# Two rows per partition, stores on a second queue, and last stores behind last loads in a windowed attention kernel

## Chip, cores, metric

One core of one Trainium2 chip. The metric is device time in microseconds (us) of one execution; each time below is the median of several executions unless it says otherwise. The runs s1 to s5 have one execution each; their times are given, but the argument reads them by their trace.

## The reference

Attention inside windows of 64 rows, in fp32. Four batches of 4,096 rows, 1,536 columns.

```python
B, S, D, W = 4, 4096, 1536, 64
q_w, k_w, v_w = (x.reshape(B, S // W, W, D) for x in (q, k, v))
logits = np.einsum('bnwd,bnud->bnwu', q_w, k_w) * D ** -0.5
attn = softmax(logits, axis=-1)                  # [cut: written out with max, exp, sum]
out = np.einsum('bnwu,bnud->bnwd', attn, v_w).reshape(B, S, D)
```

## The kernel before

It works through 128 blocks of 128 rows (two windows). Each partition holds one row. The GpSimd queue casts q, k and v from fp32 to fp16 while it loads them: one descriptor per row reads 6,144 B from HBM and writes 3,072 B to SBUF. A descriptor is the order to move one run of bytes, here one row; the trace shows one packet for each (65,536 rows in all, 65,536 data packets). Each DMA (one `dma_start`) also shows 16 completion writes of 4 B (8,192 for 512 DMAs), one for each DMA engine. TensorE transposes q and k, multiplies them, and multiplies the exponentials with v in two concurrent 64x64 quarters of the array. The stores are also issued by GpSimd, two blocks late; only the last three go through SP.

```python
    def load(blk):
        # [cut: the tiles q16, k16, v16, 3 buffers each]
        nc.gpsimd.dma_start(out=q16, in_=qb[blk].rearrange("p (c e) -> p c e", e=128))
        nc.gpsimd.dma_start(out=k16, in_=kb[blk].rearrange("p (c e) -> p c e", e=128))
        nc.gpsimd.dma_start(out=v16, in_=vb[blk])
        return q16, k16, v16
    ...
    for blk in range(NBLK):
        # [cut: first blocks are loaded ahead]
        q16, k16, v16 = load(blk)
        if len(pending_store) > 2:
            bs, ts = pending_store.pop(0)
            nc.gpsimd.dma_start(out=ob[bs], in_=ts)
        # [cut: 24 transposes, copies to SBUF]
        for c in range(DC):
            nc.tensor.matmul(lt[:, 0:128], lhsT=xt[:, 2 * c + 1, :], rhs=xt[:, 2 * c, :],
                             start=(c == 0), stop=(c == DC - 1))
        # [cut: exponentials of the two windows, row sums, reciprocal]
        for j in range(D // 512):
            nc.tensor.matmul(o[0:64, :], lhsT=et[0:64, 0:64], rhs=v16[0:64, sl], tile_position=(0, 0), ...)
            nc.tensor.matmul(o[64:128, :], lhsT=et[64:128, 64:128], rhs=v16[64:128, sl], tile_position=(64, 64), ...)
            # [cut: eviction with the reciprocal as scale]
        pending_store.append((blk, out_sb))
    for bs, ts in pending_store:
        nc.sync.dma_start(out=ob[bs], in_=ts)
```

The softmax here doesn't subtract the row's maximum and nothing guards it: scores larger than these inputs give would overflow.

Of the kernel before, what the change touches and what calls it, by code (L numbers as in the profile page):

```python
# [1 line left out]

# [4 lines left out]

FP16 = mybir.dt.float16
FP32 = mybir.dt.float32  # L10


@with_exitstack
def kernel(
    ctx: ExitStack,
    tc: tile.TileContext,
    q: bass.AP,
    k: bass.AP,
    v: bass.AP,
    out: bass.AP,  # L20
):
    nc = tc.nc

    B, S, D, W = q.shape[0], q.shape[1], q.shape[2], 64
    P = 128
    DC = D // 128
    NBLK = (B * S) // P
    scale = float(D) ** -0.5
    NPRE = 2

    qb = q.rearrange("b (n p) d -> (b n) p d", p=P)
    kb = k.rearrange("b (n p) d -> (b n) p d", p=P)
    vb = v.rearrange("b (n p) d -> (b n) p d", p=P)
    ob = out.rearrange("b (n p) d -> (b n) p d", p=P)

    consts = ctx.enter_context(tc.tile_pool(name="consts", bufs=1))
    inp = ctx.enter_context(tc.tile_pool(name="inp", bufs=3))
    xtp = ctx.enter_context(tc.tile_pool(name="xtp", bufs=2))
    etp = ctx.enter_context(tc.tile_pool(name="etp", bufs=2))
    outp = ctx.enter_context(tc.tile_pool(name="outp", bufs=6))  # L40
    rsp = ctx.enter_context(tc.tile_pool(name="rsp", bufs=2))

    tp_ps = ctx.enter_context(tc.tile_pool(name="tp_ps", bufs=2, space=bass.MemoryType.PSUM))
    lt_ps = ctx.enter_context(tc.tile_pool(name="lt_ps", bufs=2, space=bass.MemoryType.PSUM))
    o_ps = ctx.enter_context(tc.tile_pool(name="o_ps", bufs=3, space=bass.MemoryType.PSUM))
    s_ps = ctx.enter_context(tc.tile_pool(name="s_ps", bufs=1, space=bass.MemoryType.PSUM))

    exp_f = mybir.ActivationFunctionType.Exp
    copy_f = mybir.ActivationFunctionType.Copy

    def load(blk):
        q16 = inp.tile([128, DC, 128], FP16, tag="q16", name="q16")
        k16 = inp.tile([128, DC, 128], FP16, tag="k16", name="k16")
        v16 = inp.tile([128, D], FP16, tag="v16", name="v16")
        nc.gpsimd.dma_start(out=q16, in_=qb[blk].rearrange("p (c e) -> p c e", e=128))  # L55
        nc.gpsimd.dma_start(out=k16, in_=kb[blk].rearrange("p (c e) -> p c e", e=128))  # L56
        nc.gpsimd.dma_start(out=v16, in_=vb[blk])  # L57
        return q16, k16, v16

    pre = [load(blk) for blk in range(NPRE)]  # L60
    pending_store = []

    ident = consts.tile([128, 128], FP16, name="ident")
    ones = consts.tile([128, 8], FP16, name="ones")
    zeros = consts.tile([128, 1], FP32, name="zeros")
    nc.vector.memset(ident, 0.0)
    nc.vector.memset(ones, 1.0)
    nc.vector.memset(zeros, 0.0)
    nc.gpsimd.affine_select(
        out=ident,  # L70
        in_=ident,
        compare_op=mybir.AluOpType.not_equal,
        fill=1.0,
        base=0,
        pattern=[[-1, 128]],
        channel_multiplier=1,
    )

    for blk in range(NBLK):
        if blk < NPRE:  # L80
            q16, k16, v16 = pre[blk]
        else:
            q16, k16, v16 = load(blk)
        if len(pending_store) > 2:
            bs, ts = pending_store.pop(0)
            nc.gpsimd.dma_start(out=ob[bs], in_=ts)  # L86

        xt = xtp.tile([128, 2 * DC, 128], FP16, tag="xt", name="xt")
        for g in range(3):
            tp = tp_ps.tile([128, 8, 128], FP16, tag="tp", name="tp")  # L90
            for i in range(8):
                j = g * 8 + i
                c = j // 2
                src = q16[:, c, :] if (j % 2 == 0) else k16[:, c, :]
                nc.tensor.transpose(tp[:, i, :], src, ident)  # L95
            if g != 1:
                nc.vector.tensor_copy(out=xt[:, g * 8 : g * 8 + 8, :], in_=tp)  # L97
            else:
                nc.scalar.copy(out=xt[:, g * 8 : g * 8 + 8, :], in_=tp)  # L99

        lt = lt_ps.tile([128, 512], FP32, tag="lt", name="lt")
        for c in range(DC):
            nc.tensor.matmul(  # L103
                lt[:, 0:128],
                lhsT=xt[:, 2 * c + 1, :],
                rhs=xt[:, 2 * c, :],
                start=(c == 0),
                stop=(c == DC - 1),
            )

        et = etp.tile([128, 128], FP16, tag="et", name="et")
        nc.scalar.activation(  # L112
            et[0:64, 0:64], lt[0:64, 0:64], exp_f, bias=zeros[0:64], scale=scale
        )
        nc.scalar.activation(
            et[64:128, 64:128], lt[64:128, 64:128], exp_f, bias=zeros[64:128], scale=scale
        )

        sp = s_ps.tile([128, 8], FP32, tag="sp", name="sp")
        nc.tensor.matmul(  # L120
            sp[0:64, 0:1], lhsT=et[0:64, 0:64], rhs=ones[0:64, 0:1],
            tile_position=(0, 0), start=True, stop=True,
        )
        nc.tensor.matmul(  # L124
            sp[64:128, 0:1], lhsT=et[64:128, 64:128], rhs=ones[64:128, 0:1],
            tile_position=(64, 64), start=True, stop=True,
        )
        rs = rsp.tile([128, 1], FP32, tag="rs", name="rs")
        nc.vector.reciprocal(out=rs, in_=sp[:, 0:1])  # L129

        out_sb = outp.tile([128, D], FP32, tag="out_sb", name="out_sb")
        for j in range(D // 512):
            o = o_ps.tile([128, 512], FP32, tag="o", name="o")
            sl = slice(512 * j, 512 * (j + 1))
            nc.tensor.matmul(  # L135
                o[0:64, :], lhsT=et[0:64, 0:64], rhs=v16[0:64, sl],
                tile_position=(0, 0), start=True, stop=True,
            )
            nc.tensor.matmul(  # L139
                o[64:128, :], lhsT=et[64:128, 64:128], rhs=v16[64:128, sl],  # L140
                tile_position=(64, 64), start=True, stop=True,
            )
            if j % 2 == 0:
                nc.scalar.activation(out_sb[:, sl], o, copy_f, bias=0.0, scale=rs)  # L144
            else:
                nc.vector.tensor_scalar_mul(out_sb[:, sl], o, scalar1=rs)  # L146

        pending_store.append((blk, out_sb))

    for bs, ts in pending_store:  # L150
        nc.sync.dma_start(out=ob[bs], in_=ts)


# [1 line left out]
_INS = ['q', 'k', 'v']  # L155
_OUTS = [((4, 4096, 1536), 'float32')]


# [23 lines left out]
```

## Time and profile before

| | before |
|---|---|
| time, median of 3 (the result below has a fourth run) | 967.0 us (966.24 to 967.76) |
| profiled span | 964.4 us |
| TensorE busy, granted clock | 76%, 0.63 |
| bytes read and written in HBM | 302 MB, 101 MB |

The page of the kernel before: busy time of each engine; two rows of 40 time slices (granted TensorE clock and DMA busy share, in tenths); DMA packets; packets, MB and busy share by queue; HBM traffic; the chain of waits by engine. Queue q0 is GpSimd's, q1 is SP's, q8 is an instruction queue.

```profile
span 964.4 us, 14246 instructions
...
PE 731.4 (76%) x5632; PEld 510.0 (53%) x5632; DVE 294.6 (31%) x515; ACT 378.1 (39%) x641; POOL 271.1 (28%) x514
...
PEclk9776575756756666566575755766656556565655
DMA  9999999999999999999999999999999999999997
...
DMA packets 73795, 252.60 MB, mean 262 GB/s; under 512 B 8192, under 2 KB 8192, under 8 KB 73728
...
q0 software_dynamic: 73296, 249.33, 104.6%
q1 hardware_dynamic: 432, 2.36, 0.6%
q8 instruction: 44, 0.72, 0.3%
...
HBM read 301.99 MB, written 100.66 MB: 417 GB/s over the span
...
DMA 94%; issue 4%; PE 1%; POOL 0%; DVE 0%; ACT 0%; POOLq 0%; ACTq 0%; DVEq 0%
```

Read the DMA row first: 9 in every slice but the last, and the chain that ended last is 94% DMA. Then the counts. The 73,795 packets hold 65,536 data packets (65,152 on q0 and 384 on q1); most of the others are 8,192 completion writes of 4 B. The packet sizes are those of the SBUF side, so HBM traffic is larger than the "252.60 MB".

The table of stretches, with columns start:end and length, then busy us and count of each engine, then granted clock, DMA share, GB/s:

```profile
core 0: us, PE busy (x) PEld busy (x) DVE busy (x) ACT busy (x) POOL busy (x), PEclk, DMA share, GB/s
...
100.00:900.00 800.00, 620.30 (x4719) 432.69 (x4720) 246.28 (x429) 315.63 (x535) 227.99 (x429) 0.62 1.07 265
...
940.00:950.00 10.00, 8.40 (x61) 5.59 (x60) 2.95 (x6) 3.62 (x7) 0.54 (x1) 0.50 1.05 283
950.00:957.00 7.00, 4.50 (x37) 3.19 (x33) 1.92 (x3) 2.39 (x3) 0.00 (x0) 0.51 0.73 242
957.00:965.00 8.00, 1.76 (x15) 0.63 (x12) 1.13 (x3) 1.89 (x4) 0.00 (x0) 0.70 0.30 122
```

The DMA share is 1.07 in the middle (packets overlap a little) and falls to 0.73 and 0.30 at the end. Three groups of TensorE instructions (busy us, mean ns of one, then idle time ahead of them with its releaser) show what the compute side waits for:

```profile
L95 PE MATMUL tp<-ident,k 128*128 128x128 f16 x1536 | 327.7, 305 | 139.6 <-DMA k<-in_k_dram 139.6
...
L103 PE MATMUL lt<-xt 128*128 128x128 f16 x1536 | 192.9, 295 | 3.0 <-DVE xt L97 1.8
...
L135 PE MATMUL o<-v,et 64*64 64x512 f16 x384 | 150.6, 502 | 0.0
```

The transposes of k waited 139.6 us for k to arrive. TensorE is not the limit.

**The measure used below.** From the packet records of the trace I count the HBM bytes of all packets that start between 100 and 900 us (a load packet counts twice its SBUF size), and express the rate as ns per 6,144 HBM bytes and engine: 16 engines times 800,000 ns, divided by bytes/6,144. Before: 232.6 ns. The whole kernel moves 65,536 times 6,144 B, 4,096 per engine, so **1 ns of this measure is 4.1 us of kernel time**.

### The profile page before, as it was taken

What the parts mean: (1) busy time and instruction counts of PE and PEld (TensorE: products, weight loads), DVE (VectorE), ACT (ScalarE), POOL (GpSimd) and SP (SyncE); (2) the same over time, 40 slices, a digit from 0 to 9 for tenths busy, and PEclk for the clock granted to TensorE, in tenths of its full rate; (3) what the DMA queues carried; (4) which work ended last, traced back from release to release, by engine and by line L of the source; (5) the groups of instructions that cost most, each with busy time, mean ns of one, the idle gap of its engine ahead of it and who ended that gap; (6) DMA issues with size and microseconds to landing.
All of it is one profiled execution on the core that took longest, in us unless ns stands there. A gap on an engine that the chain in (4) does not pass through costs nothing.

```text
span 964.4 us, 14246 instructions
## 1 busy us (share of the span) xinstructions
PE 731.4 (76%) x5632; PEld 510.0 (53%) x5632; DVE 294.6 (31%) x515; ACT 378.1 (39%) x641; POOL 271.1 (28%) x514
## 2 busy tenths in 40 slices
PE   5667778787687877877878777777787777878775
PEld 3445555555455555555555555544555555555553
DVE  2323332333333333323233333323332323323332
ACT  3434343433333443434343433344343333344333
POOL 4222222222222222222222322322222222222220
PEclk9776575756756666566575755766656556565655
DMA  9999999999999999999999999999999999999997
GB/s 182 253 270 269 261 261 268 270 262 261 266 270 264 261 266 268 266 262 265 266 267 262 266 264 267 264 266 264 265 267 266 264 264 267 266 264 263 267 268 224
DMA packets 73795, 252.60 MB, mean 262 GB/s; under 512 B 8192, under 2 KB 8192, under 8 KB 73728
## 3 DMA queue, kind: packets, MB, share of 16 engines
q0 software_dynamic: 73296, 249.33, 104.6%
q1 hardware_dynamic: 432, 2.36, 0.6%
q8 instruction: 44, 0.72, 0.3%
q14 instruction: 23, 0.19, 0.0%
HBM read 301.99 MB, written 100.66 MB: 417 GB/s over the span
## 4 chain that ended last, share of the span: by engine, by line
DMA 94%; issue 4%; PE 1%; POOL 0%; DVE 0%; ACT 0%; POOLq 0%; ACTq 0%; DVEq 0%
DMA k<-in_k_dram 92%; DMA q<-in_q_dram 1%; PE tp L95 1%; DVE xt L97 0%; POOL q L55 0%; PE o L135 0%; PE lt L103 0%; PE o L139 0%; POOLq L56 0%; POOL v L57 0%; DVE out_sb L146 0%; ACT out_sb L144 0%; ACT et L112 0%; ACTq L177 0%; PE sp L120 0%
## 5 line engine op out<-in xcount | busy, mean ns | idle before, releaser
L95 PE MATMUL tp<-ident,k 128*128 128x128 f16 x1536 | 327.7, 305 | 139.6 <-DMA k<-in_k_dram 139.6
L95 PE MATMUL tp<-ident,q 128*128 128x128 f16 x1536 | 341.1, 296 | 28.8 <-DMA q<-in_q_dram 12.1
L95 PEld LDWEIGHTS <-k 128*128 128x128 f16 x1536 | 205.9, 139 | 205.3 <-DMA k<-in_k_dram 167.9
L97 DVE COPY xt<-tp 128x1024 f16<-128x1024 f16 x256 | 177.0, 691 | 392.4 <-PE tp L95 392.2
L95 PEld LDWEIGHTS <-q 128*128 128x128 f16 x1536 | 199.8, 137 | 89.8 <-DMA q<-in_q_dram 50.9
L99 ACT COPY xt<-tp 128x1024 f16<-128x1024 f16 x128 | 129.5, 1012 | 287.2 <-PE tp L95 287.2
L144 ACT ACTIVATE out_sb<-o,rs 128x512 f32<-128x512 f32 x256 | 168.6, 685 | 98.7 <-PE o L139 95.1
L103 PE MATMUL lt<-xt 128*128 128x128 f16 x1536 | 192.9, 295 | 3.0 <-DVE xt L97 1.8
L103 PEld LDWEIGHTS <-xt 128*128 128x128 f16 x1536 | 150.6, 136 | 27.4 <-DVE xt L97 26.5
L135 PE MATMUL o<-v,et 64*64 64x512 f16 x384 | 150.6, 502 | 0.0
L139 PE MATMUL o<-v,et 64*64 64x512 f16 x384 | 144.6, 498 | 0.0
L57 POOL DMA_DIRECT2D v<-in_v_dram x128 | 67.9, 530 | 178.1 <-DMA v<-in_v_dram 135.0
L86 POOL DMA_DIRECT2D out_dram<-out_sb x125 | 67.2, 537 | 173.5 <-DMA out_dram<-out_sb 134.0
L112 ACT ACTIVATE et<-lt,zeros 64x64 f16<-64x64 f32 x128 | 39.6, 309 | 192.4 <-PE lt L103 192.4
L56 POOL DMA_DIRECT2D k<-in_k_dram x128 | 67.9, 530 | 162.6 <-DMA k<-in_k_dram 162.6
L55 POOL DMA_DIRECT2D q<-in_q_dram x128 | 68.0, 531 | 156.2 <-PE o L139 124.0
L146 DVE TENSOR_SCALAR out_sb<-o,rs 128x512 f32<-128x512 f32 x128 | 96.0, 750 | 46.6 <-PE o L139 45.1
L129 DVE RECIPROCAL rs<-sp 128x1 f32<-128x1 f32 x128 | 21.5, 168 | 225.5 <-PE sp L124 221.0
L120 PE MATMUL sp<-ones,et 64*64 64x1 f16 x128 | 25.3, 198 | 56.5 <-ACT et L112 56.5
L120 PEld LDWEIGHTS <-et 64*64 64x64 f16 x128 | 14.4, 113 | 86.7 <-ACT et L112 86.2
L139 PEld LDWEIGHTS <-et 64*64 64x64 f16 x384 | 39.4, 132 | 16.8 <-issue 9.8
L135 PEld LDWEIGHTS <-et 64*64 64x64 f16 x384 | 43.5, 126 | 0.4
(12 smaller groups left out, 81.5 us busy)
## 6 DMA issues: line engine op xcount, KB each, us to landing
out_dram<-out_sb POOLq DMA_DIRECT2D x125, 768.0 KB, 14.2
q<-in_q_dram POOLq DMA_DIRECT2D x128, 384.0 KB, 14.3
k<-in_k_dram POOLq DMA_DIRECT2D x128, 384.0 KB, 14.3
v<-in_v_dram POOLq DMA_DIRECT2D x128, 384.0 KB, 14.3
out_dram<-out_sb SPq DMA_DIRECT2D x3, 768.0 KB, 7.8
```

The costliest lines, as they stand in the source:

```text
L55: nc.gpsimd.dma_start(out=q16, in_=qb[blk].rearrange("p (c e) -> p c e", e=128))
L56: nc.gpsimd.dma_start(out=k16, in_=kb[blk].rearrange("p (c e) -> p c e", e=128))
L57: nc.gpsimd.dma_start(out=v16, in_=vb[blk])
L86: nc.gpsimd.dma_start(out=ob[bs], in_=ts)
L95: nc.tensor.transpose(tp[:, i, :], src, ident)
L97: nc.vector.tensor_copy(out=xt[:, g * 8 : g * 8 + 8, :], in_=tp)
L99: nc.scalar.copy(out=xt[:, g * 8 : g * 8 + 8, :], in_=tp)
L103: nc.tensor.matmul(lt[:, 0:128], lhsT=xt[:, 2 * c + 1, :], rhs=xt[:, 2 * c, :], start=(c == 0), stop=(c == DC - 1),)
L135: nc.tensor.matmul(o[0:64, :], lhsT=et[0:64, 0:64], rhs=v16[0:64, sl], tile_position=(0, 0), start=True, stop=True,)
L139: nc.tensor.matmul(o[64:128, :], lhsT=et[64:128, 64:128], rhs=v16[64:128, sl], tile_position=(64, 64), start=True, stop=True,)
L144: nc.scalar.activation(out_sb[:, sl], o, copy_f, bias=0.0, scale=rs)
L146: nc.vector.tensor_scalar_mul(out_sb[:, sl], o, scalar1=rs)
```

## The change

The intent: the same bytes in half as many descriptors, each twice as long. A partition now holds two adjacent rows, so a unit is 256 rows and q, k and v descriptors read 12 KB. With two row slots, a window of 64 rows lies in 32 partitions. Scores are computed for 128 keys of one slot against 256 queries of both slots, and the value product sums over the two key slots; zeros outside the windows make full 128x128 matmuls correct. The last 256 rows are two small units of 128 rows. Loads run three units ahead. Body stores go to SP (hardware descriptors), and the last stores to GpSimd, behind the last loads.

```diff
-    def load(blk):
-        q16 = inp.tile([128, DC, 128], FP16, tag="q16", name="q16")
-        nc.gpsimd.dma_start(out=q16, in_=qb[blk].rearrange("p (c e) -> p c e", e=128))
+BODY_G, BODY_R = 1, 2
+PREFETCH = 3
+    def dram(x, u):
+        rows = x[u.row0 : u.row0 + u.rows]
+        return rows.rearrange("(g p r) d -> p g (r d)", g=u.G, p=P, r=u.R)
+    def load(u):
+        for name, src in (("q", qf), ("k", kf), ("v", vf)):
+            t = inp.tile([P, LR, D], FP16, tag=name + "16", name=name + "16")
+            dst = t[:, : u.G * u.R, :].rearrange("p (g r) d -> p g (r d)", g=u.G)
+            nc.gpsimd.dma_start(out=dst, in_=dram(src, u))
     # [cut: tiles, constants, transposes, exponentials]
-                lt[:, 0:128], lhsT=xt[:, 2 * c + 1, :], rhs=xt[:, 2 * c, :],
+                    lv[:, r, :, :], lhsT=xt[:, c, 1, r, :], rhs=xt[:, c, 0, :R, :],
-                o[0:64, :], lhsT=et[0:64, 0:64], rhs=v16[0:64, sl], tile_position=(0, 0), ...
-                o[64:128, :], lhsT=et[64:128, 64:128], rhs=v16[64:128, sl], tile_position=(64, 64), ...
+                for r in range(R):
+                    o, lhsT=et[:, r, t, :], rhs=u.v[:, g * R + r, sl], start=(r == 0), stop=(r == R - 1)
-            nc.gpsimd.dma_start(out=ob[bs], in_=ts)
-    for bs, ts in pending_store:
-        nc.sync.dma_start(out=ob[bs], in_=ts)
+                if last:    # the last unit stores in three pieces
+                    nc.sync.dma_start(out=of[u.row0 : u.row0 + u.rows, sl], in_=u.o[:, 0, sl])
+        eng = nc.gpsimd if i >= N - PREFETCH - 2 else nc.sync
+        eng.dma_start(out=dram(of, u), in_=src)
     # [cut: values of unit i-1 are computed after the scores of unit i]
```

## The prediction

> **What bounds it now.** The DMA engines. In the table of stretches their busy share is 1.07 from 100 to 900 us (packets overlap), and the chain of waits is 94% DMA, nearly all loads. The page counts 302 MB read, 101 MB written. One block (128 rows, 3.15 MB) passes every 7.42 us: 424 GB/s. Packet records: 65,536 packets of 6,144 HBM bytes, one per engine every 232.6 ns, in stretches of loads alone and of loads with stores alike. Compute engines wait: PE 76% busy although its granted clock is only 0.63; VectorE 31%, ScalarE 39%. At the start 2.6 us pass before the first packet. The last load packet ends 955 us in; the last block's compute follows, with almost no packet from 958 to 961 us, then its store. From 950 us on some 490 packets, worth 7 us, take 13 us: about 6 us lost.
>
> **What the change does.**
> - Same bytes, half the data packets, twice as long; half the completion writes. The Trainium skill ("DMA: Bandwidth & Descriptors", "Why small descriptors are slow (HBM only)") states about 3 cycles of fixed cost per packet and 32 B of metadata per operation; "Where 436 GB/s comes from" gives 32 B per cycle at 850 MHz. Estimate: 6,144 B need 226 ns, about 4.7 ns is per descriptor, the other 2 ns completion writes and instruction fetch. The measured 232.6 ns agrees; no run yet shows the split. Halving: about 229.5 ns per 6,144 B, 12 to 13 us in all, all on the critical path. That is optimistic; I count 10.5 us.
> - Stores move to the SP queue, beside the loads. Same 16 engines: no gain expected.
> - Prefetch of three 256-row units: the load queue should never run dry.
> - Tail: loads go out ahead of the last stores, so pending stores fill the last computation; the last unit has 128 rows and stores in three pieces. Of the 6 us lost, 5 return.
> - TensorE gets more: per 256 rows still 48 transposes, but 24 score matmuls 256 wide (before 128) and 12 value matmuls 128x128x512 where 12 of 64x64 ran in concurrent pairs. Timeline spacings at clock 0.5: transpose 107 ns, so 5.1 us; scores by width 213 ns, 5.1 us; values 427 ns, 5.1 us: over 15.4 us against a DMA pace of about 14.65 us per unit. All cold it would be too slow. At clock 1.0 transposes come every 56 ns and the sum is about 8 us plus waits on copies. The long matmul stretch (10 us) should lift the clock; I expect 0.7 or more, 12 to 13 us with waits, still hidden. Values of the previous unit run during this one's exponentials, removing a hidden 0.5 us wait. ScalarE: 3 copies of 1.01, 4 exponentials of 0.31, 4 evictions of 0.69: 7 us of 14.65.
>
> **Time.** 967 - 10.5 - 5 = about 951 us; 8 in 10 between 938 and 965. Faster by over 2% (under 947.7) 0.36, within 2% 0.56, slower by over 2% 0.08.
>
> **What would show it.** About 37,000 packets instead of 73,800; load packets under twice 248 ns; DMA busy share still about 1; mean rate in the middle up by 1% to 1.5%; PE busier at a higher clock, with waits on k loads remaining; no empty DMA stretch before the last store.
>
> **What would make it wrong.** If long descriptors are no cheaper per byte (HBM, not packets, sets 232.6 ns), only the tail is gained: 961. If the clock stays near 0.5, TensorE becomes the limit: 980 or more. If two queues overlap better than one, up to 20 us more are gained (floor 226 ns, about 935). Uneven engines could spoil the tail.

## The result

| | before | after |
|---|---|---|
| time, median of 4 | 966.83 us | 958.63 us (958.33 to 958.69) |
| ratio after/before | | 0.9916 (95%: 0.9901 to 0.993) |
| profiled span | 964.4 us | 956.8 us |
| ns per 6,144 HBM bytes and engine | 232.6 | 230.7 |
| last load or store packet ends | 963.2 us | 953.1 us |

A ratio here is the mean time of one kernel's runs over that of the other's of the same rounds, so not quite the ratio of the medians. The verdict is "same" at the 2% line: 8.2 us faster, inside the predicted range, but half of the predicted 16 us.

The page after:

```profile
span 956.8 us, 13110 instructions
...
PE 658.4 (69%) x5624; PEld 482.7 (50%) x5624; DVE 240.6 (25%) x392; ACT 456.1 (48%) x705; POOL 105.8 (11%) x204
...
PEclk9978889888898898888978989889988999898888
DMA  9999999999999999999999999999999999999996
...
DMA packets 37786, 252.51 MB, mean 264 GB/s; under 512 B 4192, under 2 KB 4192, under 8 KB 29664
...
q0 software_dynamic: 28656, 156.51, 78.0%
q1 hardware_dynamic: 9072, 95.16, 24.0%
q8 instruction: 44, 0.72, 0.3%
...
HBM read 301.99 MB, written 100.66 MB: 421 GB/s over the span
...
DMA 86%; PE 8%; ACT 4%; issue 1%; DVE 0%; POOL 0%; ACTq 0%; POOLq 0%; DVEq 0%
```

The packets halved, to 37,786. The SP queue q1 now carries 95 MB. DMA is still busy, up to the last slice. The granted clock rose from 0.63 to 0.88, and TensorE's busy share fell. The same stretches after:

```profile
core 0: us, PE busy (x) PEld busy (x) DVE busy (x) ACT busy (x) POOL busy (x), PEclk, DMA share, GB/s
...
100.00:900.00 800.00, 559.13 (x4753) 410.30 (x4751) 202.26 (x324) 384.09 (x595) 85.62 (x162) 0.88 1.03 267
...
940.00:950.00 10.00, 5.70 (x51) 3.12 (x49) 3.62 (x7) 7.03 (x12) 1.06 (x2) 1.00 0.75 314
950.00:957.00 7.00, 0.00 (x0) 0.00 (x0) 0.00 (x0) 0.00 (x0) 0.00 (x0) 0.54 0.42 160
957.00:965.00 8.00, 0.00 (x0) 0.00 (x0) 0.00 (x0) 0.00 (x0) 0.00 (x0) 0.88 0.00 0
```

The mean rate in the middle rose from 265 to 267 GB/s only. The last 17 us are still thin (0.75 and 0.42), and no engine computes after 950 us although the span ends at 956.8. The TensorE groups that answer those of before:

```profile
L140 PE MATMUL tp<-ident,k 128*128 128x128 f16 x1536 | 259.6, 270 | 172.9 <-DMA k<-in_k_dram 172.9
...
L198 PE MATMUL o<-v,et 128*128 128x512 f16 x762 | 185.1, 378 | 61.5 <-ACT out_sb L204 61.4
...
L165 PE MATMUL lt<-xt 128*128 128x256 f16 x1512 | 188.4, 277 | 0.5
```

Transposes of k still wait for k, now 172.9 us in all, so TensorE stayed hidden in spite of its wider products. The score matmuls are twice as wide and take 277 ns each instead of 295; the value matmuls fill the array and take 378 ns instead of 502. That fits the higher clock; what raised the clock was not tested. The issue table (KB each, median us from issue to landing):

```profile
out_dram<-out_sb SPq DMA_DIRECT2D x60, 1536.0 KB, 11.4
q<-in_q_dram POOLq DMA_DIRECT2D x63, 768.0 KB, 40.4
...
out_dram<-out_sb POOLq DMA_DIRECT2D x3, 1536.0 KB, 9.1
```

A store of 1.5 MB on SP lands 11.4 us after issue. A load that reads as much from HBM (768 KB in SBUF) needs 40.4 us: it queues behind the loads issued ahead of it, and the stores on SP pass it by. Three of the last large stores go through GpSimd, as planned.

### Where the 8 us come from

From the packet records: time lost against a kernel's own middle rate, in us. "Closing" is from the end of the last packet to the end of the span.

```
                     before    after    change
middle rate x bytes    952.8    945.1     -7.7     (4,096 x 232.61 or 230.74 ns)
start to 100 us          4.3      3.8     -0.5
from 900 us on           6.1      4.2     -1.9
closing                  1.2      3.8     +2.5
sum                    964.4    956.8     -7.6     (spans 964.4 and 956.8)
```

(The changes are worked out before rounding.)

The closing is explained by the records of GpSimd's last instructions, which the profile does not count as busy:

```
before: last GpSimd packet 958.9; last data landed 963.6; GpSimd DRAIN ends 962.8; span ends 964.4
after:  last GpSimd packet 951.6; last data landed 953.4; GpSimd DRAIN ends 956.1; span ends 956.8
```

After the change all data had landed at 953.4 us, and the program waited 2.6 us more for GpSimd's closing DRAIN. Before, the drain ended ahead of the last data.

### The profile page after: what moved, and what is told of

Its sections match the earlier page's. It is cut to its first block, busy times and chain, and to the rows that moved or that the text cites. A ratio compares the mean times of both kernels' runs of the same rounds, so it can differ in the third digit from the quotient of the medians.

```text
span 956.8 us, 13110 instructions
## 1 busy us (share of the span) xinstructions
PE 658.4 (69%) x5624; PEld 482.7 (50%) x5624; DVE 240.6 (25%) x392; ACT 456.1 (48%) x705; POOL 105.8 (11%) x204
## 4 chain that ended last, share of the span: by engine, by line
DMA 86%; PE 8%; ACT 4%; issue 1%; DVE 0%; POOL 0%; ACTq 0%; POOLq 0%; DVEq 0%
DMA k<-in_k_dram 40%; DMA v<-in_v_dram 40%; DMA q<-in_q_dram 6%; PE tp L140 3%; PE lt L165 3%; ACT xt L147 2%; PE o L198 2%; ACT et L177 1%; ACT out_sb L204 1%; DVE xt L145 0%; PE lt L126 0%; PE sp L187 0%; POOL q L84 0%; ACTq L257 0%; POOL v L84 0%
## 5 line engine op out<-in xcount | busy, mean ns | idle before, releaser
L140 PE MATMUL tp<-ident,k 128*128 128x128 f16 x1536 | 259.6, 270 | 172.9 <-DMA k<-in_k_dram 172.9
L147 ACT COPY xt<-tp 128x1024 f16<-128x1024 f16 x192 | 194.3, 1012 | 348.3 <-PE tp L140 348.3
L140 PE MATMUL tp<-ident,q 128*128 128x128 f16 x1536 | 253.6, 264 | 52.1 <-ACT xt L147 21.4
L140 PEld LDWEIGHTS <-k 128*128 128x128 f16 x1536 | 156.8, 125 | 184.0 <-DMA k<-in_k_dram 183.8
L198 PE MATMUL o<-v,et 128*128 128x512 f16 x762 | 185.1, 378 | 61.5 <-ACT out_sb L204 61.4
L165 PE MATMUL lt<-xt 128*128 128x256 f16 x1512 | 188.4, 277 | 0.5
L177 ACT ACTIVATE et<-lt,zeros 32x128 f16<-32x128 f32 (+1 forms) x256 | 91.8, 358 | 124.5 <-PE sp L187 114.6
L198 PEld LDWEIGHTS <-et 128*128 128x128 f16 x762 | 69.0, 96 | 146.9 <-issue 79.2
L187 PEld LDWEIGHTS <-et 128*128 128x128 f16 x254 | 15.7, 97 | 1.9 <-ACT et L177 0.5
L216 POOL DMA_DIRECT2D out_dram<-out_sb x4 | 2.1, 532 | 25.2 <-ACT out_sb L204 22.3
L126 PE MATMUL lt<-xt 128*128 128x128 f16 x24 | 2.4, 221 | 2.6 <-ACT xt L147 1.7
## 6 DMA issues: line engine op xcount, KB each, us to landing
out_dram<-out_sb SPq DMA_DIRECT2D x60, 1536.0 KB, 11.4
q<-in_q_dram POOLq DMA_DIRECT2D x63, 768.0 KB, 40.4
```

Of the source, the lines that this page charges most:

```text
L126: nc.tensor.matmul(lv[:, r, :, :], lhsT=xt[:, c, 1, r, :], rhs=xt[:, c, 0, :R, :], start=(c == 0), stop=(c == DC - 1),)
L140: nc.tensor.transpose(tp[:, c - c0, x, r, :], src[:, g * R + r, c * P : (c + 1) * P], ident)
L147: nc.scalar.copy(out=dst, in_=tp)
L165: nc.tensor.matmul(lv[:, r, :, :], lhsT=xt[:, c, 1, r, :], rhs=xt[:, c, 0, :R, :], start=(c == 0), stop=(c == DC - 1),)
L177: nc.scalar.activation(et[s, :, :, s], lv[s, :, :, s], EXP, bias=zeros[s], scale=scale)
L187: nc.tensor.matmul(sp[:, t, 0:1], lhsT=et[:, r, t, :], rhs=ones[:, 0:1], start=(r == 0), stop=(r == R - 1),)
```

## Experiments

My theories after the result: (1) the middle gain is a fixed cost per descriptor; (2) SP stores beside loads cost something, since 1-us bins of the changed kernel with loads alone run at 428 GB/s of HBM traffic and mixed bins at 424 to 425; (3) GpSimd's drain lengthens the end. Rivals stand with each run. Experiments e1 to e4 and s1 to s4 ran on chip 12 (kernel before: 966.28 us for e1 to e4, one run of 966.05 beside s1 to s4); s5 and e5 to e7 ran on chip 6 (966.28).

### e1: the changed kernel with 6 KB descriptors

```diff
-BODY_G, BODY_R = 1, 2
+BODY_G, BODY_R = 2, 1
```

> The changed kernel with units of two 128-row groups: 6 KB descriptors again, but units, prefetch, number of DMA instructions, completion writes, queues and tail as in the changed kernel. Theory (the gain in the steady part, 230.7 against 232.6 ns per 6,144 HBM bytes and engine from 100 to 900 us, is the fixed cost per descriptor): back to 232 to 233 ns, time 965 to 967 us. Rival (store queue, deeper prefetch, or fewer DMA instructions made the gain): stays at 230.5 to 231 ns, time 957 to 960 us. TensorE does less work here, its clock falls below 0.8.

Measured: 969.2 us (ratio to before 1.0027), 234.1 ns, clock 0.80. The page of e1:

```profile
DMA packets 70043, 252.49 MB, mean 261 GB/s; under 512 B 4192, under 2 KB 4192, under 8 KB 69984
...
q0 software_dynamic: 53232, 156.51, 80.6%
q1 hardware_dynamic: 16752, 95.16, 24.9%
```

The packets doubled again while the number of DMA instructions stayed, and the whole gain was gone: with the stores on SP, the prefetch, the larger units and the second queue together gain nothing without the longer descriptors. That does not show that none of them gains by itself (e7 finds one that does). It was 1.5 ns worse than even the kernel before, which theory (1) had not said: something else in the changed kernel costs.

### e2: body stores back on the GpSimd queue

```diff
-        eng = nc.gpsimd if i >= N - PREFETCH - 2 else nc.sync
+        eng = nc.gpsimd
```

> The changed kernel with the body stores on the GpSimd queue again, behind loads. Theory (descriptor size alone makes the steady gain): 230.7 ns stays, time within 2 us of 958.6. Rival A (the second queue overlaps packets better and made the gain): 232 ns, 964 us or more. Rival B (mixing two queues costs: in the changed kernel 1-us bins of loads alone run at 428 GB/s of HBM traffic, mixed bins at 424 to 425): mixed bins rise to 428, time about 954 us.

Measured: 953.9 us (ratio 0.9871), 229.8 ns; bins with 40 to 60% stores rose from 424.4 to 427.8 GB/s. The queues of e2:

```profile
DMA packets 37786, 252.51 MB, mean 265 GB/s; under 512 B 4192, under 2 KB 4192, under 8 KB 29664
...
q0 software_dynamic: 37296, 250.89, 101.9%
...
q1 hardware_dynamic: 432, 0.79, 0.2%
```

The packets are as many, nearly all on q0, and the kernel is about 5 us faster than the changed one (958.5 us on chip 6, 958.6 at first). Rival B was right: the second queue cost 0.9 ns, 3.7 us. My theory ("within 2 us of 958.6") missed.

### e4: the kernel before with its stores on SP

```diff
-            nc.gpsimd.dma_start(out=ob[bs], in_=ts)
+            nc.sync.dma_start(out=ob[bs], in_=ts)
```

> The kernel before with its stores issued on SP, nothing else changed. Theory (a second queue gives nothing in the steady part): 232 to 233 ns per 6,144 bytes; the time changes by less than 3 us, by its tail alone. Rival (the second queue is part of the gain): 231 ns or less and 960 us or less.

Measured: 976.8 us (ratio 1.0107), 234.8 ns. The stretch from 100 to 900 us of e4:

```profile
100.00:900.00 800.00, 522.52 (x4678) 377.78 (x4675) 244.91 (x426) 303.67 (x532) 169.95 (x321) 0.73 1.07 262
```

262 GB/s against 265 before. Theory and rival were both wrong: the second queue does not help and is not neutral; it cost 2.2 ns (9 us), and the tail the rest. With twice as many store packets it cost about twice what it does in the changed kernel.

**Where it shows.** Durations of the store packets in the traces, 100 to 900 us except where noted:

```
kernel                          stores on  12 KB: 460 ns / 473 ns    6 KB: 234 ns / 247 ns
before                          GpSimd                                12,021 / 1,718
e4 (whole run, loads present)   SP                                     1,854 / 14,203
after                           SP         781 / 6,117
e2                              GpSimd     6,057 / 874
```

A store packet takes 13 ns longer when it stands beside a load packet. The size fits: had none of the 13 ns been hidden, the 5,243 more long packets of the changed kernel than of e2 would cost 1.2 ns per 6,144 B, and the 10,318 more of e4 than of the kernel before (12,036 in the same stretch) 2.5 ns; 0.9 and 2.2 were measured. On one queue a store runs as a batch, and about one packet per engine and store is the long one. On two queues nearly all are long. This agrees with the Trainium skill ("DMA: Bandwidth & Descriptors", "Queues, rings and completion order"), which says that an engine takes turns between the queue rows it has work for, packet by packet. Here a packet is one descriptor.

### s5: alternate loads and stores on one queue

Is it the change of direction, or the SP queue? A kernel of the same DMA traffic alone (wrong result, described at s1 below), all on GpSimd, with each store cut into 8 pieces of 16 partitions, set between pieces of the loads (in outline):

```diff
-        order = [(gpsimd, load) for q, k, v] + [(gpsimd, store)]
+        order = load[0:48], store[0:16], load[48:96], store[16:32], ...   # 9 load and 8 store pieces
```

> DMA-only, two rows per descriptor, everything on the GpSimd queue, but each unit's store cut into 8 pieces of 16 partitions (one packet per engine) set between pieces of the loads, so that an engine goes from load to store to load packet by packet on one queue. If it is the change of direction that costs (store packets of 460 ns that follow a store, 473 ns beside loads): most store packets at 473 ns, about 0.8 ns more per 6,144 bytes beyond the cost of four times as many completion writes. If it is the SP queue itself: store packets stay at 460 ns.

Measured: 7,825 of 8,192 store packets took 473 ns; in s2, the same traffic with whole stores, 992 did and 7,199 took 460 ns. So the SP queue is not needed for it: the long store packet is the one that follows a load, on either kind of queue. A rival fits s5 as well, since each of its store pieces has one packet per engine: the long packet could be the first of any DMA. s2 speaks against it. Its 992 long packets are 62 stores times 16 engines; the last two of its 64 stores follow another store and not a load, and all 305 store packets after the last load took 460 ns.

The run's rate (237.2 ns, against 228.9 for s2) is no measure of the cost, and the 0.8 ns that I expected can't be read from it: 13,312 more completion writes account for about 3.5 ns (worked out at e7) and the longer stores for some 1.4 ns (13 ns for about 7,000 more of them, over 65,536). The rest, 3.4 ns, stays unexplained; the trace shows 655 load packets of over 500 ns between 100 and 900 us, where s2 has 28, about 3.8 ns per 6,144 B in excess time.

### e3: the last unit but one stores through SP

```diff
-        eng = nc.gpsimd if i >= N - PREFETCH - 2 else nc.sync
+        eng = nc.gpsimd if N - PREFETCH - 2 <= i < N - 2 else nc.sync
```

> The changed kernel with only the store of the last unit but one moved from GpSimd to SP. Theory (the closing drain of GpSimd ends about 4.5 us after the last packet of its own queue, and after 951.6 us that puts the end at 956.8 although all data had landed at 953.4): the drain ends before the data, the span ends about 0.9 us after the last landing, time 2 to 2.5 us less than 958.6. Rival (the drain's length has nothing to do with this store; the end is bound by the last data): no change, within 0.5 us.

Measured: 956.0 us (ratio 0.9892), about 2.6 us less than the changed kernel. The drain ended at 953.2 us instead of 956.1, still just behind the last data (953.0) and not ahead of it as I expected. Theory (3) holds. How far the drain trails is not a constant: over all fourteen traces it ended 1.3 (s3) to 5.3 us (s5) after the last packet of GpSimd's own queue. What sets that stays open.

### s1, s2, s3: the DMA traffic alone with 6, 12 and 24 KB descriptors

These kernels only load q, k and v with the cast and store constants, all on GpSimd, with no matmuls. A store waits for its unit's loads through a one-column VectorE copy. Their outputs are wrong, which doesn't matter for the times. The loads have 6, 4 and 3 buffers.

```diff
-R = 1     # s1: one row per partition, 6 KB in HBM
+R = 2     # s2: 12 KB
+R = 4     # s3: 24 KB
```

> Wrong result on purpose: only the loads and stores of the kernel (all on the GpSimd queue, one row per descriptor, constants stored), no matmuls. Per-descriptor theory: near the 232.6 ns per 6,144 HBM bytes and engine of the kernel before, perhaps 0.5 ns less because no instructions are fetched for TensorE; load packets 248, stores 234 ns. Skew: in the kernel before, the first and the last of the 16 engines' completions of one DMA drift apart from 0.4 us at 15 us to 7.5 us at 933 us. If instruction fetches cause that (44 fetches of 16 KB, 0.94 us each), it stays under 2 us here; if some engines are slower by themselves, it reaches 6 us or more again.

> The same with two rows per descriptor (12 KB in HBM). Per-descriptor theory: 2.5 to 3 ns less per 6,144 bytes than with one row, so 229 to 230 ns; 474 and 460 ns packets. Rival (the gain of the longer descriptors came from fewer DMA instructions, other buffering or the compute engines): within 0.7 ns of the one-row run. Skew as in the one-row run: under 2 us if instruction fetches cause it.

> The same with four rows per descriptor (24 KB in HBM). A fixed cost per descriptor halves again: 1.2 to 1.5 ns less than with two rows, 227.5 to 228.7 ns. Rival (the cost is per byte beyond 12 KB, or long descriptors are cut up): no gain over two rows, or the packet count does not halve.

Measured, one execution each: 963.96, 949.11 and 942.06 us; 231.8, 228.9 and 227.5 ns. Span and packets on the pages of s1, s2 and s3:

```profile
span 962.2 us, 1450 instructions
...
DMA packets 73739, 251.78 MB, mean 262 GB/s; under 512 B 8192, under 2 KB 8192, under 8 KB 73728
```

```profile
span 947.3 us, 746 instructions
...
DMA packets 36870, 251.72 MB, mean 266 GB/s; under 512 B 4096, under 2 KB 4096, under 8 KB 28672
```

```profile
span 940.3 us, 394 instructions
...
DMA packets 18435, 251.69 MB, mean 268 GB/s; under 512 B 2048, under 2 KB 2048, under 8 KB 2048
```

The packet counts halve each time, and the savings are 2.9 and then 1.4 ns: what a fixed cost that is shared by twice the bytes does. The number of DMAs halves along with the descriptors, so this cost is that of both; e7 will part them. The line through s1 and s2 is 226.1 ns plus 5.8 ns divided by the rows per descriptor; for four rows it gives 227.49, and 227.55 was measured. The 226.1 ns is 27.2 B per ns and engine, which is the figure of the Trainium skill ("DMA: Bandwidth & Descriptors", "Where 436 GB/s comes from": 32 B per cycle at 850 MHz). The traffic with 24 KB descriptors ran at 432 GB/s of HBM bytes.

On the spread of the engines my expectation was half wrong: the first and the last of the 16 completions of one DMA stood 3 to 4 us apart at the end, not under 2 and not 6 or more.

### s4: s2 with 5,632 dummy matmuls

The tail of both kernels is thin because the 16 engines do not finish together. In the kernel before, the 16 completions of one DMA, in us after the first of them:

```
at  15 us: 0  0.06 0.14 0.15 0.16 0.19 0.22 0.23 0.24 0.28 0.29 0.32 0.36 0.37 0.41 0.44
at 451 us: 0  0.03 0.08 0.63 0.66 1.42 1.64 1.68 2.78 2.84 2.87 2.92 2.94 3.11 3.93 4.08
at 918 us: 0  0.03 0.06 0.61 0.64 2.74 2.94 3.76 6.07 6.22 6.28 6.34 6.35 6.37 6.45 6.52
```

Eight engines fall steadily behind. The q8 line of the page offers a suspect: 0.72 MB of instructions in 44 packets of 16 KB, about 0.94 us each, evenly over the run. It is TensorE's stream: 11,264 matmuls and weight loads in 0.72 MB are 64 B each. s4 adds that stream to s2 and nothing else of weight:

```diff
+            # [in outline: the file has a constant, FILL, that goes from 0 to 88]
+            for f in range(88):
+                nc.tensor.matmul(pt[:, 0:P], lhsT=w, rhs=w if f else ts[2][:, 0:P], start=(f == 0), stop=(f == 87))
```

> The two-row DMA-only kernel plus 88 dummy matmuls per unit (5,632 in all, each with a weight load: the instruction count of TensorE in the kernel before, about 0.72 MB of instruction fetches). If instruction fetches drive the engines apart: the spread of the 16 completions reaches 5 to 9 us at the end, 8 or so engines ahead of the others, and the time is 3 to 6 us longer than without the dummies. If not: spread and time as in the run without them.

Measured, one execution: 954.3 us, 5.2 us more than s2; the spread of the completions at the end 8.0 us instead of 3.0; middle rate 229.7 ns instead of 228.9. From the page of s4:

```profile
span 952.4 us, 12072 instructions
...
q8 instruction: 44, 0.72, 0.3%
```

So work on an engine that is not the limit, with its stream of instructions, cost 5 us of DMA time: 3.0 us through the mean rate (0.73 ns) and the rest at the end, where the engines ahead have nothing left to do. The dummies did not hold up the loads, which landed 29.0 us after issue in both runs (medians). The trace does not name the engine of a packet, so that the fetches fall on just the eight slow ones is inferred, not shown. An estimate from the trace fits it: 44 fetches of 0.94 us are 41 us; on eight engines that is 5.2 us each, and the spread grew by 5.0. s4 adds TensorE's work along with its fetches and does not part the two.

### e5, e6, e7: both findings together, and the descriptor alone on one queue

e5 is the changed kernel again. e6 keeps body stores on GpSimd and sends the last two units' stores through SP:

```diff
-        eng = nc.gpsimd if i >= N - PREFETCH - 2 else nc.sync
+        eng = nc.gpsimd if i < N - 2 else nc.sync
```

e7 is e6 with `BODY_G, BODY_R = 2, 1`.

> The changed kernel unaltered, beside the other two on the same chip: 958 to 959 us.

> The changed kernel with both findings: body stores on the GpSimd queue behind loads, the stores of the last two units on SP. Theory (one queue avoids changes of direction; the GpSimd drain ends earlier): 951.5 to 953 us, steady 229.8 ns, the span ends under 1.5 us after the last packet. Rival (the two gains do not add): 954 us or more.

> e6 with 6 KB descriptors (units of two 128-row groups), nothing else changed. Descriptor theory on one queue: 2.8 to 2.9 ns more per 6,144 bytes than e6, so 11 to 12 us more: 963 to 965 us. Rival (the prefetch, fewer completion writes and the tail make a good part of the gain): 960 us or less.

Measured in the same rounds: before 966.28, e5 958.52 (ratio 0.9920), e6 953.09 (0.9863), e7 958.32 (0.9917). The page of e6:

```profile
span 951.4 us, 13105 instructions
...
q0 software_dynamic: 37152, 250.10, 101.8%
q1 hardware_dynamic: 576, 1.57, 0.4%
...
DMA 97%; issue 1%; PE 0%; ACT 0%; POOL 0%; POOLq 0%; ACTq 0%
```

e6 beats both kernels. It ran 229.8 ns and ended 1.2 us after its last packet; its time is just above the 951.5 to 953 us that I expected. The chain is 97% DMA. Of the two findings the queue gave nearly all: e6 is only 0.8 us faster than e2, whose drain had already ended close behind the data.

The page of e7:

```profile
DMA packets 70043, 252.49 MB, mean 264 GB/s; under 512 B 4192, under 2 KB 4192, under 8 KB 69984
...
q0 software_dynamic: 69408, 250.10, 105.1%
```

e7 missed my expectation of 963 to 965 us (its rival, 960 or less, was right), and tells the parts of the saving apart. From e6 to e7 only the descriptors halve in length: 231.53 against 229.75 ns, 1.78 ns. So one descriptor costs about 3.6 ns, near the roughly 3 cycles per packet of the Trainium skill ("DMA: Bandwidth & Descriptors", "Why small descriptors are slow (HBM only)"), which would be 3.5 ns at 850 MHz (an estimate). The rest of the 2.9 ns between s1 and s2, 1.1 ns, is what is left for the halved number of DMAs, and the step from the kernel before to e7, which halves the DMAs with 6 KB descriptors throughout (and changes units, prefetch and TensorE's work), is the same 1.1 ns. Each engine had 4 DMAs with a completion write each for 32 data packets of 6,144 B and now has 2, so one DMA is worth about 17 ns on an engine (1.08 times 32/2). Most of it should be the completion write, which no run isolates; an estimated 3 ns is the long first packet of each store (13 ns in one DMA of four). The trace agrees in size: completion writes took 9 or 22 ns, 18.9 on average in the kernel before. With its larger units, deeper prefetch and new tail, e7 brings the kernel from 966 to 958 us without any longer descriptor.

## Why the prediction was right, and where it was off

The time fell inside the range (938 to 965), the likeliest class was right, and the limit was read correctly. The centre, 951, was 7.6 us low because two terms were mis-sized, both in the same direction; a range 27 us wide covered that. The number alone would have misled: 958.6 lies nearer to the 961 that I had named for descriptors that gain nothing than to 951, although the longer descriptors and fewer DMAs did gain what I had counted for them.

- **"The DMA engines" bound it; TensorE "still hidden", clock "0.7 or more".** Right. The clock was 0.88, and k waits remained. "PE busier" was wrong: its busy share fell from 76% to 69%, with about as many instructions, some of them wider, at a higher clock. The middle rate rose by 0.8%, not by the "1% to 1.5%" that was to show it.
- **"About 4.7 ns is per descriptor, the other 2 ns completion writes and instruction fetch ... I count 10.5 us."** The mechanism and size were right on one queue: from the kernel before to e2 the rate fell by 2.8 ns, 11.3 us. Of the split, the descriptor came out smaller, 3.6 ns instead of 4.7, and the rest larger: 2.1 ns for the DMAs with their completion writes per 6,144 B in the kernel before, and 0.7 ns for instruction fetches in s4.
- **"Stores move to the SP queue, beside the loads. Same 16 engines: no gain expected."** This step failed first. I took it as zero; it cost 0.9 ns, 3.7 us, by setting nearly every store packet behind a load packet (e2, e4, s5). The upside I had named for it, "if two queues overlap better than one", has the wrong sign.
- **"Of the 6 us lost, 5 return."** This step failed second. In the DMA time 1.9 us returned and in the closing 2.5 us were added: net +0.6. The order of stores did what I meant it to: before, no load or store packet was in flight for 2.0 us from 959.1 us on; after, the longest such gap from 930 us on is 0.14 us. But part of the loss was never the order of stores but engines that drift apart (s4), which a store order cannot mend. Stores that end late on the GpSimd queue bring its drain to the end of the program (e3).

Sum: -11.3 (descriptors and completions) + 3.7 (second queue) + 0.6 (end) - 0.5 (start) = -7.6 us of span (worked out before rounding), as measured.

## What to carry to other kernels

In a DMA-bound kernel, first ask for ns per byte and engine in the middle, then what stands between that and 226 ns per 6 KB: here 3.6 ns per descriptor, about 17 ns per DMA and engine, up to 13 ns per store packet that stands beside a load packet, and instruction fetches. Make descriptors long, DMAs few, and let loads and stores follow each other in batches on one queue rather than interleave from two. At the end, look past the last packet, and at the spread of the 16 completions, before rearranging the last stores.

## What the Trainium skill lacked or had wrong

- "DMA: Bandwidth & Descriptors", "Issuing engines are not separate DMA queues", says that the queues run on the same engines and that more issuing engines save only sequencer time. It lacks that stores on a second queue beside loads cost time: 953.9 to about 958.6 us here with 12 KB descriptors, 966.3 to 976.8 us with 6 KB.
- The same page has no cost for a change between load and store packets: 13 ns per store packet (460 to 473, 234 to 247 ns), on a GpSimd queue too (s5).
- The same page, "Bandwidth": its largest figure for loads is 425 GB/s (97%). Loads and stores with 24 KB descriptors ran at 432 GB/s here, and going from 12 to 24 KB still gained 7 us of 949.
- The same page, "Latency and other measured facts", calls engines 7 and 15 usually slower and guesses at descriptor rings. Here eight of the 16 completions trailed by 6 to 8 us after 900 us, and dummy matmuls with 0.72 MB of instruction fetches raised the spread from 3.0 to 8.0 us (s2, s4). The time that instruction fetches take on the DMA engines (44 of 0.94 us here) would belong to "Runtime: NRT & Kernel Launch", "Instruction fetch mechanics", which does not have it.
- No page I read has the closing drain of GpSimd: it ended 1.3 to 5.3 us after the last packet of its own queue and set the end of the changed kernel.
- "Why small descriptors are slow (HBM only)" agrees in size: its roughly 3 cycles per packet would be 3.5 ns at 850 MHz (an estimate), and 3.6 ns were measured between 6 and 12 KB packets. It names no cost of a DMA's completion write (about 17 ns per DMA and engine, all told); "Anatomy of one DMA" calls the semaphore write itself essentially free.
